# An unequal split of tokens over eight cores, with one program per kind of core behind a branch

## The chip, the cores and the metric

The kernel runs on the 8 cores of one Trainium2 chip, as one launch. Cores 0 to 3 are one die, 4 to 7 the other. Each core has a matrix engine (TensorE, PE), a vector engine (VectorE, DVE), a scalar engine (ScalarE, ACT), GpSimd (POOL) and a sync engine (SyncE, SP), which here does nothing but issue copies (DMAs).

The metric is the device time of the slowest core, in microseconds (us). The three fast runs of the kernel before lie within 0.1% of each other (1601.88 to 1602.89 us), those of the changed kernel within 0.2% (1641.26 to 1644.21). Some executions fall into a slower state in which a die runs at a lower granted clock: the changed kernel had one run of 1760.98 us in which all cores of die 0 were near clock 0.90 (0.883 to 0.904), where its fast runs have 0.958 to 0.983 on that die. A "look" is one profiled execution with its time; a run "with rounds" was also timed in turns with the kernel before, on the same chip.

## The reference

One decoder layer on `x` of shape (2, 4096, 2048). An input projection of 16384 columns gives q, k and v of three groups of 8 attention heads, gates, and the input of a pooling branch. Cut to what matters here:

```python
DILATED_GROUPS = ((128, 1), (512, 4), (2048, 16))   # (window, dilation)
...
for g, (window, dilation) in enumerate(DILATED_GROUPS):
    # query t attends to t, t-d, t-2d, ..., t-window
    o_g, lse_g = dilated_window_attention(qg, kg, v[:, :, g], window, dilation)
...
x = x + jnp.einsum('bsd,de->bse', merged, w_out)
```

Group 2 looks back 2048 tokens. A core that holds a stretch of a sequence therefore needs the keys and values of up to 2048 tokens before it, its *halo*, and computes them itself from x. Groups 0 and 1 need at most the last 512 of these.

## The kernel before

Each sequence is cut into four equal parts, one for each of four cores: 1024 own tokens, 2048 halo tokens. All eight cores run one program. Where the halo lies before the start of the sequence, its x is zero and a mask removes it.

The projections are sums over 16 blocks of 128 input features: matmuls of 128 weight columns against up to 512 tokens. A small scheduler written in Python orders the instructions of all engines when the kernel is built, one list for each engine.

In stage 1 the keys and values of group 2 go through DRAM, because they are needed later, sorted by their position modulo 16. Values are computed in tiles of 128 tokens x 512 columns (4 heads); each tile is copied out of PSUM by ACT, and stored by one copy that SP issues:

```python
def value_tile(qd, t, i):
    vi = yield ("acq", P_vst)                       # one of 3 staging tiles
    yield ("op", "act", act_us(512), lambda a: a.copy(out=vst[vi][:], in_=ps[i][:]), [B_ps[i]], [B_vst[vi]])
    F.release(P_pp, i)
    yield ("dma", "sp", 131e3, lambda s: s.dma_start(
        out=v2d[4 * qd:4 * qd + 4, :, t, :].rearrange("h p c -> p h c"),
        in_=vst[vi][:].rearrange("p (h c) -> p h c", h=4)), [B_vst[vi]], [B_v2d[(qd, t)]], f"vs{vi}")
```

In stage 2, attention, each head's keys and values of group 2 are loaded back:

```python
def load_k2(h, i):
    ...
    ("dma", "sp", 786e3, lambda s: s.dma_start(out=v2[i][:], in_=v2d[h]), ...)
    ("dma", "sp", 786e3, lambda s: s.dma_start(out=k2[i][:], in_=k2d[h]), ...)
```

The rotary embedding of keys and queries needs the two halves of 32 rows swapped. That is done by two small copies on the same SP queue, which here are called the *swap*:

```python
def rope(pool, rots, B_rots, tag, st, B_st, n, tb, B_tb, t0):
    ...
    def swap(hf):
        yield ("dma", "sp", 40e3, lambda s: s.dma_start(
            out=rb[32 + 16 * hf:48 + 16 * hf, 0:n], in_=st[16 - 16 * hf:32 - 16 * hf, 0:n]), ...)
```

Stages 3 to 5 (pooling, gates, output projection) are streams of matmuls with weights loaded by POOL's queue.

## Time and profile before

1602.32 us, the median of three fast runs (1601.88 to 1602.89). The profile:

| what | value | view |
|---|---|---|
| PE busy | 1537.1 us of 1605.8 (96%) | page, part 1 |
| chain that ended last | 92% PE | page, part 4 |
| PE busy, 280 to 1500 us | 1219.95 of 1220 us, clock 1.00 | windows |
| PE busy, 0 to 280 us | 221.51 of 280 us, clock 0.84 | windows |
| first load of x issued | 1.06 us | timeline |

The page of the kernel before, part 2: the span in 40 slices, each digit the busy tenths of one slice, and the granted clock in tenths.

```profile
PE   3699987999999999999999999999999999999997
...
PEclk9778888999999999999999999999999999999999
```

The windows of the slowest core of the kernel before; the columns are the stretch in us, then busy us and number of instructions for PE, weight loads, DVE, ACT and POOL, then clock, DMA share and GB/s.

```profile
0.00:280.00 280.00, 221.51 (x833) 90.79 (x834) 153.32 (x231) 155.86 (x221) 99.94 (x80) 0.84 0.57 146
280.00:1500.00 1220.00, 1219.95 (x6499) 622.34 (x6498) 482.82 (x741) 414.33 (x713) 73.42 (x139) 1.00 0.43 82
```

After the start-up the PE has practically no gap: whatever removes matmul columns there shortens the kernel, as long as nothing new makes the PE wait. The price of a matmul is read from the timeline of PE (core 2; start, duration, then the group):

```profile
512.40 2.76 PE L734 MATMUL ps<-s_hX,s_w_56 128*128 128x384 bf16 x16
515.00 0.33 PE L751 MATMUL ps<-s_sq_50,s_ones 128*128 128x384 bf16 x1
...
525.48 3.62 PE L734 MATMUL ps<-s_hX,s_w_56 128*128 128x512 bf16 x16
528.93 0.38 PE L751 MATMUL ps<-s_sq_50,s_ones 128*128 128x512 bf16 x1
```

From start to start, 16 matmuls of 384 columns take 2.60 us and 16 of 512 take 3.45 us. That is 162.5 and 215.8 ns a matmul, and both fit columns / 2.4 ns plus 2.5 ns.

In the middle of attention (600 to 680 us, core 1) the swap copies of queries land in 1.9 to 2.7 us; the columns are the copy, its count, KB each, and median us from issue to landing:

```profile
s_k_88<-k2d SPq DMA_DIRECT2D x1, 768.0 KB, 4.7
s_v_89<-v2d SPq DMA_DIRECT2D x1, 768.0 KB, 4.8
s_rotb_103<-s_qS_101 SPq DMA_DIRECT2D x4, 32.0 KB, 1.9
...
s_rotb_104<-s_qT_111 SPq DMA_DIRECT2D x2, 32.0 KB, 2.7
```

### The profile page before, as it was taken

To read this page: it belongs to the slowest core of one execution; us is meant where nothing else is said; L and a number is where in the kernel's file an instruction comes from. 1 tells how busy PE (TensorE), PEld (TensorE's weight loads), DVE (VectorE), ACT (ScalarE), POOL (GpSimd) and SP (SyncE) were. 2 spreads that over 40 slices of the span, in tenths; PEclk is the share of its full clock that TensorE was granted. 3 is DMA by queue.
4 is the path that set the end of the run, shared out by engine and by line. 5 is a ranking of instruction groups with operands and counts; after the bars stand their busy time and mean duration, and the time that the engine had idled before them with its cause. 6 is when DMAs were issued, how large, how long until landed. Compare 5 with 4: busy or idle time off the path is not lost.

```text
span 1605.8 us, 23141 instructions; the slowest of 8 cores (1596.8 to 1605.8 us)
## 1 busy us (share of the span) xinstructions
PE 1537.1 (96%) x7772; PEld 756.3 (47%) x7772; DVE 655.5 (41%) x999; ACT 570.2 (36%) x932; POOL 176.5 (11%) x225
## 2 busy tenths in 40 slices
PE   3699987999999999999999999999999999999997
PEld 1234433445645455555555555564444444444443
DVE  5457266423000477675027676675322222221221
ACT  3654476323111556664146665521111111111000
POOL 1033645001000000000000000000000000000000
PEclk9778888999999999999999999999999999999999
DMA  9953532117142644443354443434444444444883
GB/s 204 195 166 107 157 101 87 54 48 144 43 117 47 109 99 91 84 99 80 53 93 84 91 98 63 85 67 94 72 74 77 79 79 76 73 76 79 192 215 106
DMA packets 80468, 158.87 MB, mean 99 GB/s; under 512 B 33824, under 2 KB 41888, under 8 KB 80352
## 3 DMA queue, kind: packets, MB, share of 16 engines
q0 software_dynamic: 23184, 84.42, 31.6%
q1 hardware_dynamic: 56544, 72.51, 14.9%
q8 instruction: 65, 1.06, 0.3%
q10 hardware_dynamic: 624, 0.46, 0.1%
q14 instruction: 51, 0.42, 0.1%
HBM read 216.27 MB, written 20.97 MB: 148 GB/s over the span
## 4 chain that ended last, share of the span: by engine, by line
PE 92%; DMA 2%; issue 2%; DVE 2%; ACT 1%; SPq 0%; DVEq 0%; ACTq 0%
PE ps L734 69%; PE ps L1445 7%; PE ps L1395 7%; PE ps L845 3%; PE ps L751 2%; PE ps L1081 1%; PE ps L1116 1%; PE ps L1120 1%; DMA s_xs_63<-xc 1%; DMA s_rota_78<-s_kst_74 1%; PE ps L678 1%; PE ps L1301 0%; DMA s_rota_78<-s_kst_71 0%; DVE s_acc L674 0%; DMA s_rota_78<-s_kst_72 0%
## 5 line engine op out<-in xcount | busy, mean ns | idle before, releaser
L734 PE MATMUL ps<-s_hX,s_w_56 128*128 128x512 bf16 (+3 forms) x3712 | 801.4, 368 | 0.0
L734 PEld LDWEIGHTS ps<-s_hX,s_w_56 128*128 128x128 bf16 x3712 | 364.1, 98 | 375.7 <-issue 13.3
L578 POOL DMA_DIRECT2D s_w_56<-wst x152 | 80.4, 530 | 1228.0 <-PE ps L734 878.9
L734 PE MATMUL ps<-s_w_56,s_hX 128*128 128x512 bf16 x672 | 147.2, 379 | 0.0
L1445 PE MATMUL ps<-s_mT,s_w_56 128*128 128x512 bf16 x512 | 110.7, 379 | 0.0
L734 PEld LDWEIGHTS ps<-s_w_56,s_hX 128*128 128x128 bf16 x672 | 71.6, 107 | 71.5
L760 DVE SCALAR_TENSOR_TENSOR s_kS_107<-ps,s_cst,s_rr_51 128x384 bf16<-128x384 f32 x8 | 4.9, 615 | 182.7 <-PE ps L734 178.6
L1445 PEld LDWEIGHTS ps<-s_mT,s_w_56 128*128 128x128 bf16 x512 | 50.1, 98 | 60.4
L755 ACT ACTIVATE s_rr_52<-ps 128x512 f32<-128x512 f32 (+1 forms) x72 | 42.6, 591 | 66.7 <-PE ps L751 57.8
L755 ACT ACTIVATE s_rr_51<-ps 128x512 f32<-128x512 f32 (+1 forms) x72 | 41.4, 575 | 68.1 <-PE ps L751 64.7
L734 PE MATMUL ps<-s_w_57,s_hTh_54 128*128 128x512 bf16 x256 | 63.1, 408 | 0.0
L734 PE MATMUL ps<-s_w_57,s_hTh_55 128*128 128x512 bf16 x256 | 61.9, 408 | 0.0
L1395 PE MATMUL ps<-s_pT,s_w_56 128*128 128x512 bf16 x256 | 60.5, 379 | 0.0
L1395 PE MATMUL ps<-s_aT,s_w_56 128*128 128x512 bf16 x256 | 60.5, 379 | 0.0
L748 ACT ACTIVATE s_sq_49<-ps 128x512 bf16<-128x512 f32 (+1 forms) x72 | 42.0, 584 | 40.2 <-PE ps L734 38.7
L734 PE MATMUL ps<-s_w_57,s_hX 128*128 128x512 bf16 x256 | 55.6, 379 | 0.0
L748 ACT ACTIVATE s_sq_50<-ps 128x512 bf16<-128x512 f32 (+1 forms) x72 | 41.7, 580 | 33.7 <-PE ps L734 32.8
L751 PE MATMUL ps<-s_sq_49,s_ones 128*128 128x512 bf16 (+1 forms) x72 | 27.6, 383 | 22.5 <-ACT s_sq_49 L748 21.6
L758 ACT ACTIVATE s_rr_52<-s_rr_52 128x512 f32<-128x512 f32 (+1 forms) x72 | 44.5, 618 | 5.5
L758 ACT ACTIVATE s_rr_51<-s_rr_51 128x512 f32<-128x512 f32 (+1 forms) x72 | 43.6, 606 | 6.1 <-ACT s_rr_51 L755 0.4
L734 PEld LDWEIGHTS ps<-s_w_57,s_hX 128*128 128x128 bf16 x256 | 36.7, 143 | 18.6
L734 PEld LDWEIGHTS ps<-s_w_57,s_hTh_54 128*128 128x128 bf16 x256 | 26.5, 103 | 35.5 <-issue 20.7
(299 smaller groups left out, 1620.1 us busy)
## 6 DMA issues: line engine op xcount, KB each, us to landing
s_w_56<-wst POOLq DMA_DIRECT2D x152, 512.0 KB, 5.2
s_w_57<-wst POOLq DMA_DIRECT2D x8, 512.0 KB, 10.2
s_xs_58<-xc SPq DMA_DIRECT2D x6, 512.0 KB, 5.9
s_xs_59<-xc SPq DMA_DIRECT2D x6, 512.0 KB, 5.6
s_xs_60<-xc SPq DMA_DIRECT2D x6, 512.0 KB, 6.0
s_xs_61<-xc SPq DMA_DIRECT2D x6, 512.0 KB, 7.3
s_xs_62<-xc SPq DMA_DIRECT2D x6, 512.0 KB, 7.6
s_xs_63<-xc SPq DMA_DIRECT2D x6, 512.0 KB, 8.0
```

Of the source, the lines that this page charges most:

```text
L578: yield ("dma", "pool", 1048576, lambda g: g.dma_start(out=wsl[pos][:].rearrange("p k n -> p (k n)"), in_=wst[k]), after, [B_w[pos]], f"w{ ...
L678: yield ("op", "pe", 1.0, lambda t, ax=ax: t.matmul(ps[ax][:], lhsT=onesf[:], rhs=acc[:], start=True, stop=True), [B_acc, B_onesf], [B_ps[ ...
L734: yield ("op", "pe", mm_us(n), lambda t, kc=kc, a=lhs(kc), b=rhs(kc): t.matmul(ps[i][:, 0:n], lhsT=a, rhs=b, start=(kc == 0), stop=(kc == ...
L748: yield ("op", "act", act_us(n), lambda a: a.activation(out=sq[si][:, 0:n], in_=ps[i][:, 0:n], func=AF.Square), [B_ps[i]], [B_sq[si]])
L751: yield ("op", "pe", mm_us(n), lambda t: t.matmul(ps[ax][:, 0:n], lhsT=ones[:], rhs=sq[si][:, 0:n], start=True, stop=True), [B_sq[si], B_o ...
L755: yield ("op", "act", act_us(n), lambda a: a.activation(out=rr[ri][:, 0:n], in_=ps[ax][:, 0:n], func=AF.Ln, bias=float(128 * EPS)), [B_ps[ ...
L758: yield ("op", "act", act_us(n), lambda a: a.activation(out=rr[ri][:, 0:n], in_=rr[ri][:, 0:n], func=AF.Exp, scale=-0.5), [B_rr[ri]], [B_r ...
L845: yield ("op", "pe", mm_us(512), lambda t, kc=kc, b=mov(kc): t.matmul(ps[i][:], lhsT=w["t"][:, kc, :], rhs=b, start=(kc == 0), stop=(kc == ...
L1081: yield ("op", "pe", mm_us(n), lambda t, kap=kap, qap=qap, e0=e0, n=n: t.matmul(ps[si][:, e0:e0 + n], lhsT=kap, rhs=qap, start=True, stop= ...
L1116: yield ("op", "pe", mm_us(n), lambda t, vap=vap, e1=e1, cc=cc, n=n, k=k: t.matmul(nu[:, cc:cc + n], lhsT=vap, rhs=Eb[ei][:, e1:e1 + n], s ...
L1395: b=src[:, h, t0:t0 + n]: t.matmul(ps[yi][:, 0:n], lhsT=a, rhs=b, start=(h == 0), stop=(h == 7)), w["bufs"] + [B_src[h]], [B_ps[yi]])
L1445: b=mT[:, db, t0:t0 + n]: t.matmul(ps[i][:, 0:n], lhsT=a, rhs=b, start=(db == 0), stop=(db == KC - 1)), w["bufs"] + [B_mT[db]], [B_ps[i]])
```

## The change

The first core of a sequence computes 2048 halo tokens that do not exist, the second 1024. The change gives these cores more own tokens and no such halo: 1168 tokens and no halo, 1008 with 1168 halo tokens, and twice 960 with 2048. The program is built three times, and each engine picks its arm by a word loaded from DRAM.

```diff
+KINDS = ((1168, 0), (1008, 1168), (960, 2048))
+KIND = (0, 1, 2, 2)
+START = (0, 1168, 2176, 3136)
...
+        def arms(name, eng):
+            reg = eng.alloc_register("kind_" + name)
+            eng.reg_load(reg, io["kind"])
+            for k in eng.Switch(eng.snap(reg), n=len(KINDS)):
+                runs[k](name, eng)
...
 def value_tile(qd, t, i, nr):
     yield ("dma", "sp", 131e3, lambda s: s.dma_start(
-        out=v2d[4 * qd:4 * qd + 4, :, t, :].rearrange("h p c -> p h c"),
-        in_=vst[vi][:].rearrange("p (h c) -> p h c", h=4)), ...
+        out=v2d[4 * qd:4 * qd + 4, 0:nr, t, :].rearrange("h p c -> p h c"),
+        in_=vst[vi][0:nr].rearrange("p (h c) -> p h c", h=4)), ...
...
 def load_k2(h, i):
+    if H:
+        part(lambda s: s.dma_start(out=k2[i][:, 0:2048].rearrange("p (r l) -> p r l", r=16)[:, :, 0:Hr],
+                                   in_=k2d[h, :, 0:H].rearrange("p (r l) -> p r l", r=16)), ...)
+        part(lambda s: s.dma_start(out=k2[i][:, 2048:2048 + T], in_=k2d[h, :, H:H + T]), ...)
+        part(lambda s: s.dma_start(out=v2[i][0:Hr, 0:16, :], in_=v2d[h, 0:Hr, 0:16, :]), ...)
+    ...
+    part(lambda s: s.dma_start(out=v2[i][0:nr, t0:NV2, :], in_=v2d[h, 0:nr, t0:NV2, :]), ...)
...
```

(Sizes become functions of the kind; matmul pieces follow, 400 tokens instead of 512 and so on.) With 16 positions modulo 16, a value tile of the no-halo core, and a halo tile of the 1008-token core, has 1168 / 16 = 73 rows. The own tiles of the other kinds have 126 and 120 rows, and the halo tiles of the 960-token cores still 128.

## The prediction

> **What bounds the kernel now.** TensorE, by the columns it streams. The page gives PE 96% busy and a chain that is 92% PE. The table of windows gives PE 1219.95 us busy of the 1220 us from 280 to 1500 us, at granted clock 1.00. The loss is elsewhere: before 280 us the PE idles and reruns at a reduced clock (0.75 to 0.87), waiting for x, for the sums of squares (two waits, 32.3 us), and for ACT behind copies of late tokens (8.8 us each); and about 10 us of tail follow the last matmul. In the timeline, 16 matmuls of 512 columns take 3.45 us (215.8 ns each) and 16 of 384 take 2.60 us (162.5 ns): both are columns/2.4 ns + 2.5 ns[...]. Over all matmuls of the program this sums to 1495 us; the other 108 us of 1603 are start and tail.
>
> Every core does the same work, although the first core of each sequence computes keys and values for 2048 halo tokens that do not exist, and the second for 1024 such.
>
> **What the change does, by the same sum over each arm (estimates from those two durations).**
> - 1168 tokens, no halo: 8843 matmuls, 1423 us.
> - 1008 + 1168 halo: 7638 matmuls, 1428 us.
> - 960 + 2048 halo: 7638 matmuls, 1432 us.
>
> The split is well balanced, and the slowest kind saves 1495 - 1432 = 63 us. Only some 3 us of this lie in the first 280 us of the 960-token core (its halo chunks stay 512 columns); the rest lies where the PE has no gap, so nearly all is on the critical path.
>
> Added: each engine loads a word from DRAM and branches into one of three arms. [...] The first x load, now issued at 1.06 us, should come near 5 to 7 us, and everything moves with it: +5 us (a guess). Zero-filling of halo keys on POOL and four reloads per head instead of two lie off the path. Weights are needed faster (one 512 KB block per 6.5 us rather than 6.9), but a block lands in 5.2 us with several in flight and DMA is 44% busy, so it holds. The last stage, with DMA 0.8 busy, will be near 0.85.
>
> **Cores.** The 960-token cores keep today's start-up loss: 1603 - 63 + 5 = 1545. The 1008-token cores have less matmul work to hide the start behind, but shorter loads; same loss assumed: 1540. The no-halo cores have no late copies and perhaps half the loss: about 1490. ACT, DVE and POOL element counts fall or stay in all arms, so they should not take over.
>
> **Predicted: 1544 us**, 8 in 10 between 1524 and 1565. Faster by over 2%: 0.92; within 2%: 0.07; slower: 0.01.
>
> **What would show it.** No-halo cores end 40 us or more before the others; the other six end within 15 us of each other. PE busy near 1470 us on the slowest. No PE gaps from about 280 us on. First DMA issue near 6 us.
>
> **What would make it wrong.** A longer start on the 1008-token core (ACT and DVE chains no longer hidden), new PE gaps in attention from shorter pieces and the single accumulation bank, the last stage hitting DMA limits, a branch that costs tens of us[...].

## More of the kernel before

What the prediction did not look at is the value stores. On core 1 of the kernel before (issue time on SP in ns, min/median/max, and last the time from issue to landing of all copies that touch this tensor):

```profile
L827 SPq DMA_DIRECT2D v2d<-s_vst_75 x16: 360/371/977, 127.5 to 433.6; - x16
...
DMA to landing us min/median/max: 1.9/2.0/12.7
```

A store of 128 rows occupies SP for 0.37 us.

## The result, and the profile after

The changed kernel takes 1643.38 us, the median of its three fast runs (1641.26 to 1644.21), against 1602.32 before. The ratio is 1.0253, 95% interval 1.023 to 1.0277: slower by 2.5%. Executions in which one die ran at a lower clock are left out of the means. (Ratios here are the mean time of one kernel's fast runs over that of the other's in the same rounds, so not quite the ratio of the medians.)

The spans of the cores show at once where to look:

```profile
core 0: 1591.4 us, clock 0.971
core 1: 1632.6 us, clock 0.961
core 2: 1548.5 us, clock 0.983
core 3: 1548.0 us, clock 0.983
core 4: 1588.7 us, clock 0.972
core 5: 1641.7 us, clock 0.959
core 6: 1543.7 us, clock 0.983
core 7: 1548.2 us, clock 0.981
```

The 960-token cores (2, 3, 6, 7) are where the prediction had them (1545). The 1008-token cores (1, 5) are 93 and 102 us later than predicted, the no-halo cores (0, 4) some 100. PE busy on the slowest core is 1470.3 us, near the prediction; the time is in waits. The page of that core (5), part 2, to be held against the one above:

```profile
PE   2576679977999989879999798999999999999997
...
PEclk9788789998999999989999899999999999999999
```

There are more gaps in stage 1 (the first 10 slices), and gaps in attention that were not there before, and the clock dips beside them. The waits of PE on core 1 (who, for whom; us in total, times, longest):

```profile
PE ps L835 <- ACT s_sq_143 L832: 27.1, 2, 16.8
...
PE ps L757 <- POOL s_acc L753: 20.8, 2, 18.0
PE ps L1275 <- DVE s_qT_154 L870: 15.4, 2, 8.6
PE ps L1275 <- DVE s_qT_155 L870: 11.7, 2, 6.1
...
PE ps L1275 <- DVE s_qS_202 L870: 5.1, 1, 5.1
```

The same core of the kernel before has no wait for rope, and this one for POOL:

```profile
PE ps L678 <- POOL s_acc L674: 5.3, 1, 5.3
```

L1275 is the score matmul of attention and L870 the last step of rope: attention waits for rotated queries. L757 (L678 before) waits for sums of squares of x that came late. DVE and POOL wait in their turn; the copies show for what. First the value stores on core 0, where all of them have 73 rows, as in the view above:

```profile
L913 SPq DMA_DIRECT2D v2d<-s_vst_80 x11: 387/3973/4077, 146.8 to 282.2; - x11
L913 SPq DMA_DIRECT2D v2d<-s_vst_81 x11: 233/3946/4105, 162.3 to 290.4; - x11
```

Where such stores follow one another, each holds SP for 4 us, ten times as long as one of 128 rows, though it moves 43% less. That is longer than the 3.45 us of the tile's matmuls, so stores pile up. On core 1 other copies stand between the stores: most stores take SP only 0.3 to 0.4 us, and the hold falls on the copy issued next. SP's timeline in stage 1 shows it; loads of x (L715), issued right after a store, take 4.6 and 5.3 us of SP instead of the 0.33 us that others take:

```profile
144.21 5.25 SPq L715 DMA_DIRECT2D s_xs_160<-xc  x1
...
150.02 0.34 SPq L913 DMA_DIRECT2D v2d<-s_vst_175  x1
150.51 4.61 SPq L715 DMA_DIRECT2D s_xs_161<-xc  x1
```

Then attention, core 1, 640 to 670 us, around a reload, to be held against the four lines before:

```profile
s_k_188<-k2d SPq DMA_DIRECT2D x1, 292.0 KB, 4.7
s_v_189<-v2d SPq DMA_DIRECT2D x1, 292.0 KB
...
s_rotb_204<-s_qT_154 SPq DMA_DIRECT2D x2, 31.5 KB, 14.6
```

The swap issued after the reload lands after 14.6 us, where the same swap (of `s_qT`) took 2.7 before. The DVE waits for it (10.5 us idle at 666 us), and the PE for the DVE (8.6 us idle at 669 us).

### The profile page after: what moved, and what is told of

Same layout as the page of the kernel before. It is cut to its first block, busy times and chain, and to the rows that moved or that the text cites. A ratio compares the mean times of both kernels' runs of the same rounds, so it can differ in the third digit from the quotient of the medians.

```text
span 1641.7 us, 22964 instructions; the slowest of 8 cores (1543.7 to 1641.7 us)
## 1 busy us (share of the span) xinstructions
PE 1470.3 (90%) x7644; PEld 786.1 (48%) x7644; DVE 599.7 (37%) x999; ACT 534.8 (33%) x924; POOL 153.7 (9%) x231
## 4 chain that ended last, share of the span: by engine, by line
PE 75%; DMA 9%; SPq 7%; issue 3%; DVE 3%; ACT 1%; POOL 1%; ACTq 0%; DVEq 0%; POOLq 0%
PE ps L818 56%; PE ps L1619 7%; PE ps L1569 7%; SPq L857 3%; SPq L913 2%; DMA s_rotb_204<-s_qT_154 2%; DMA s_rotb_203<-s_qT_155 2%; PE ps L1275 2%; PE ps L1301 1%; SPq L903 1%; PE ps L835 1%; DMA s_rotb_203<-s_qS_202 1%; POOL s_acc L753 1%; PE ps L1305 1%; DMA s_rota_179<-s_kst_171 1%
## 5 line engine op out<-in xcount | busy, mean ns | idle before, releaser
L818 PE MATMUL ps<-s_w_156,s_hX 128*128 128x512 bf16 (+2 forms) x672 | 147.1, 379 | 0.0
L818 PEld LDWEIGHTS ps<-s_w_156,s_hX 128*128 128x128 bf16 (+2 forms) x672 | 82.5, 123 | 60.8
L1619 PE MATMUL ps<-s_mT,s_w_156 128*128 128x496 bf16 (+1 forms) x512 | 109.0, 376 | 0.0
L839 ACT ACTIVATE s_rr_144<-ps 128x512 f32<-128x512 f32 (+3 forms) x72 | 38.0, 528 | 92.2 <-PE ps L835 65.1
L1569 PE MATMUL ps<-s_aT,s_w_156 128*128 128x512 bf16 (+1 forms) x256 | 59.6, 376 | 0.0
L1569 PE MATMUL ps<-s_pT,s_w_156 128*128 128x512 bf16 (+1 forms) x256 | 59.6, 376 | 0.0
L818 PE MATMUL ps<-s_w_157,s_hX 128*126 128x512 bf16 x256 | 59.5, 394 | 0.0
L818 PEld LDWEIGHTS ps<-s_w_157,s_hX 128*126 128x126 bf16 x256 | 59.2, 323 | 0.3
L839 ACT ACTIVATE s_rr_145<-ps 128x512 f32<-128x512 f32 (+3 forms) x72 | 38.8, 539 | 59.1 <-PE ps L835 52.9
L818 PE MATMUL ps<-s_w_157,s_hTh_147 128*73 128x512 bf16 x256 | 57.8, 383 | 0.0
L818 PE MATMUL ps<-s_w_157,s_hTh_148 128*73 128x512 bf16 x256 | 57.3, 384 | 0.0
L757 PE MATMUL ps<-s_acc,s_onesf 128*128 128x292 f32 (+2 forms) x12 | 7.9, 762 | 53.9 <-DVE s_acc L753 35.0
L832 ACT ACTIVATE s_sq_142<-ps 128x512 bf16<-128x512 f32 (+3 forms) x72 | 38.1, 529 | 39.2 <-PE ps L818 38.3
L832 ACT ACTIVATE s_sq_143<-ps 128x512 bf16<-128x512 f32 (+3 forms) x72 | 38.4, 534 | 32.9 <-PE ps L818 30.0
## 6 DMA issues: line engine op xcount, KB each, us to landing
s_w_157<-wst POOLq DMA_DIRECT2D x8, 512.0 KB, 10.5
```

The lines of the kernel that those rows point to most:

```text
L818: yield ("op", "pe", mm_us(n), lambda t, kc=kc, a=lhs(kc), b=rhs(kc): t.matmul(ps[i][0:nr, 0:n], lhsT=a, rhs=b, start=(kc == 0), stop=(kc ...
L832: yield ("op", "act", act_us(n), lambda a: a.activation(out=sq[si][:, 0:n], in_=ps[i][:, 0:n], func=AF.Square), [B_ps[i]], [B_sq[si]])
L839: yield ("op", "act", act_us(n), lambda a: a.activation(out=rr[ri][:, 0:n], in_=ps[ax][:, 0:n], func=AF.Ln, bias=float(128 * EPS)), [B_ps[ ...
L1569: b=src[:, h, t0:t0 + n]: t.matmul(ps[yi][:, 0:n], lhsT=a, rhs=b, start=(h == 0), stop=(h == 7)), w["bufs"] + [B_src[h]], [B_ps[yi]])
L1619: b=mT[:, db, t0:t0 + n]: t.matmul(ps[i][:, 0:n], lhsT=a, rhs=b, start=(db == 0), stop=(db == KC - 1)), w["bufs"] + [B_mT[db]], [B_ps[i]])
```

## Experiments

**Theory A.** A copy of 73 rows is served by a single DMA engine out of 16, and so takes longer than one of 128 rows that is spread over them. Which other row counts would be quick or slow was the author's estimate, and the runs below test it. No view names the engines of a copy, but the consequences can be tested, and the packets of the kept traces bear on it (after before_64_64 below). From 204 to 232 us SP of core 0 issues nothing but these stores; its queue then (packets, MB, share of 16 engines' time):

```profile
q1 hardware_dynamic: 1987, 0.51, 8.0%
```

That is 18 GB/s, and 8.0% of 16 engines is 1.3 engines (never more than two packets overlap). An estimate: 73 KB in 4.07 us is 18.4 GB/s, so by theory A the 292 KB of a reload of 73 rows would keep one engine busy for 16 us, close to the 14.6 us of the swap behind it.

**Theory B.** The key reload of the 1008-token cores writes 16 pieces of 146 bytes in each partition, 2048 small pieces, and these delay the swaps.

**Theory C.** It has nothing to do with copies: these cores have less matmul work to hide the start behind, and the shorter pieces make attention's chains longer. This was the prediction's own worry.

All runs gave correct results but the two marked as wrong. A span can differ between fast runs of the same program by some 10 us (core 1 of the changed kernel: 1632.6, 1637.2 and 1642.6; core 5 only 1638.5 to 1641.7), so differences below that are not read. Gains below are counted from the look at the changed kernel, whose core 1 is the lowest of the three.

### split_all: 73 rows as 64 and 9, stores and reloads

```diff
+def row_parts(n):
+    return [(0, 64), (64, 73)] if n == 73 else [(0, n)]
...
-    s.dma_start(out=v2d[4 * qd:4 * qd + 4, 0:nr, t, :]..., in_=vst[vi][0:nr]...)
+    for r0, r1 in row_parts(nr):        # each with its own semaphore
+        s.dma_start(out=v2d[4 * qd:4 * qd + 4, r0:r1, t, :]..., in_=vst[vi][r0:r1]...)
...                                      # both value reloads in load_k2 in the same way
```

> Every 73-row copy of values (stores to DRAM in stage 1, reloads in stage 2, on the no-halo and the 1008-token cores) is issued as 64 rows and 9 rows; nothing else changes. Theory A (a copy of 73 rows is served by one DMA engine of the 16, so it holds the sync queue and the rope swaps behind it): the 1008-token cores fall from 1633-1642 us to 1550 (+-15), the no-halo cores from 1590 to about 1520, the 960-token cores stay at 1544-1549, and the program takes about 1550 us, faster than before by some 3%. A store no longer takes 4 us on the sync queue. Theory B (146-byte pieces of the key reload delay the swaps): the store part gains something at most, attention gaps (33 us) remain on the 1008-token cores, nothing moves much: 1610 or more. Theory C (less matmul work to hide the start behind, shorter attention pieces): no change, 1635-1645 us.

1558.07 us median against 1602.14 before: ratio 0.971 (0.966 to 0.976), **faster by 2.9%**. The 1008-token cores took 1555.2 and 1556.2 us, the no-halo cores 1535.6 and 1535.1, the others 1542.5 to 1550.3. The stores of core 1, and then its longest waits of PE:

```profile
L927 SPq DMA_DIRECT2D v2d<-s_vst x80: 308/607/1046, 113.4 to 406.1; - x80
```

```profile
PE ps L764 <- DVE s_acc L760: 33.5, 2, 26.3
PE ps L842 <- ACT s_sq L839: 28.9, 5, 10.1
PE ps L952 <- DVE s_hTh L795: 11.1, 5, 3.8
PE ps L764 <- POOL s_acc L760: 7.2, 2, 4.4
```

No store occupies SP for over 1.05 us, and the waits of attention for rope (the three of L1275 above, 32 us) are gone; the queries' swaps at 640 to 670 us land in 2.1 us. Theory C falls as the cause of this loss: the matmul pieces are unchanged here. The windows of PE on core 1 divide the gain; first the changed kernel, then split_all:

```profile
0.00:410.00 410.00, 291.26 (x1464) 0.90 0.42 98
410.00:1100.00 690.00, 657.02 (x3730) 0.98 0.39 73
```

```profile
0.00:410.00 410.00, 327.02 (x1619) 0.93 0.45 103
410.00:1100.00 690.00, 688.22 (x3938) 1.00 0.44 80
```

36 us of PE time come back in stage 1 (327.02 - 291.26) and 31 us in attention (688.22 - 657.02), and the mean clock is higher in both (0.93 after 0.90, 1.00 after 0.98), where there are fewer gaps.

### split_stores and split_loads: one half of it each

The same edit, for the stores alone and for the reloads alone.

> Only the stores of 73 rows are split into 64 and 9; the reloads stay. Theory A: the part of the loss before 410 us goes, about 50 us of the 1008-token cores (to about 1590) and 45 us of the no-halo cores (to about 1545); the gaps of attention between 500 and 1100 us stay. Theories B and C: unchanged within 10 us.

1607.3 us. Core 1 took 1605.7 us (27 less than in the changed kernel), core 0 1568.8 (23 less). The direction is as theory A has it, the sizes are about half of what was expected, and the attention gaps stay as expected. The waits for rope stay (26.3 and 11.7 us on core 1), and swaps after a reload land after 7 to 10 us in the median.

> Only the reloads of 73 rows are split; the stores stay. Theory A: the swaps that follow a reload land in 2 to 4 us and no longer in 14.6, the attention gaps (33 us of PE idle on the 1008-token cores, 26 us on the no-halo cores) go, and the cores end some 35 and 30 us sooner: 1600 and 1560. Theory B: the no-halo cores, which have no 146-byte pieces, gain; the 1008-token cores do not.

1593.79 us. Core 1 took 1591.6 us (41 less), core 0 1553.9 (37 less): somewhat more than expected. No wait for rope is left on core 1, and the queries' swaps land in 2.0 to 2.4 us; the late sums of squares stay (POOL 20.6 us). The 1008-token cores gain although their 146-byte pieces are still there, which speaks against theory B. So the reloads cost more than the stores on all four cores (0 and 4, 1 and 5), the reverse of what was expected; together they account for 68 of the 77 us that split_all wins on core 1.

### k2_compact: theory B by itself

```diff
-    s.dma_start(out=k2[i][:, 0:2048].rearrange("p (r l) -> p r l", r=16)[:, :, 0:Hr], in_=k2d[h, :, 0:H]...)
+    s.dma_start(out=k2[i][:, 0:H], in_=k2d[h, :, 0:H])
...
-    ks[:, 128 * (r + 8 * bb):128 * (r + 8 * bb) + 128]
+    ks[:, Hr * (r + 8 * bb):Hr * (r + 8 * bb) + 128]      # the mask removes what lies past Hr
```

> The key reload of the 1008-token cores is made contiguous (2336 bytes a partition instead of 16 pieces of 146 bytes); the 73-row copies stay. Theory A: the 1008-token cores gain less than 8 us and the swap behind a reload still takes over 10 us. Theory B: the swap lands in 2 to 4 us and the 1008-token cores gain 30 to 40 us (to about 1600). The other cores are the same program, so unchanged in both.

1645.3 us, cores 1 and 5 at 1643.6 and 1643.4: nothing gained. The waits for rope on core 1 are 33.1 and 5.2 us, and the swap behind a reload (640 to 680 us) is as late as ever:

```profile
s_k<-k2d SPq DMA_DIRECT2D x1, 292.0 KB, 4.4
...
s_rotb<-s_qT SPq DMA_DIRECT2D x2, 31.5 KB, 16.1
```

Theory B falls.

### both_fixed: the small pieces again, without the 73-row copies

split_all and k2_compact together.

> The 64+9 rows of split_all and the contiguous key reload together. With the one-engine copies gone, theory B is asked again for what is left of it: if the 146-byte pieces still delay anything on the path, the 1008-token cores gain 5 us or more over split_all (1555-1556 us); if not, less than 3 us, and the program stays at 1553-1558 us. Either way faster than before by about 3%.

1555.99 us median, ratio 0.9713 (0.9696 to 0.9729), the 1008-token cores at 1553.5 and 1554.5 us: some 2 us under those of split_all, which ran on another chip. The small pieces cost nothing that can be told apart here.

### split_71_2: a control

```diff
-    return [(0, 64), (64, 73)] if n == 73 else [(0, n)]
+    return [(0, 71), (71, 73)] if n == 73 else [(0, n)]
```

> A control for split_all: the same two copies in place of one, with the same semaphores and order, but cut 71 + 2 instead of 64 + 9. [...] theory A says that the large part stays on one engine and nothing is won: the 1008-token cores 1625-1650 us, the no-halo cores 1585-1600. If the gain of split_all came from having two copies, or from the changed schedule, it comes here too: about 1556.

1654.85 us, cores 1 and 5 at 1653.2 and 1645.4, cores 0 and 4 at 1601.1 and 1594.6, two of the four by up to 3 us above theory A's ranges. Two copies, the same semaphores, the same order of issue, and nothing is won. So the gain of split_all is neither the second copy nor a luckier schedule. One store held SP for 19.8 us.

### split_62_11: a dose

`(0, 62), (62, 73)`.

> The dose: the 73-row copies cut 62 + 11, [...] with the same number of copies in each case. Theory A: [...] most of the loss goes: the 1008-token cores between 1560 and 1580 us. If any row number that is no multiple of 16 were as bad as 73, about 1645.

1568.11 us, cores 1 and 5 at 1565.3 and 1566.4. Most of the loss is gone, and some 10 us more are left than with 64 + 9 (four runs of split_all: 1555.2 to 1557.3 on these cores), among them 6 us of waits for rope on core 1. That most of the loss would go was the author's estimate; on core 1 the stores of both parts held SP for 0.43 us in the median and 4.46 us at most. Between large parts of 71 rows (1653), 62 (1565) and 64 (1555) the number of rows alone was changed, and the time of core 1 falls as the 4-byte packets that a pair of copies sends rise (3, 13 and 25, counted below). The three ran on three chips, on which the kernel before took 1602 us each time.

### t1152: other constants, no copy split

```diff
-KINDS = ((1168, 0), (1008, 1168), (960, 2048))
+KINDS = ((1152, 0), (1024, 1152), (960, 2048))
-START = (0, 1168, 2176, 3136)
+START = (0, 1152, 2176, 3136)
```

> The changed kernel with other constants only: 1152 tokens without halo, 1024 with 1152 halo tokens, twice 960 with 2048. Rows per value tile become 72 (no halo, and halo of the second core) and 128 (own tiles of the second core); no copy is split. Theory A [...] no store takes 4 us on the sync queue; the columns of the 1024-token cores sum to 1443 us against 1428, so those cores should take 1556 + 15 = 1571 us, the no-halo cores 1535 - 22 = 1513, the 960-token cores 1544-1550. If what counts is any row number that is not a multiple of 16, or the small halo itself (theory C), the 1024-token cores stay above 1630 us.

1565.3 us median, ratio 0.9768 (0.9752 to 0.9785): faster by 2.3%, from three constants. Cores 1 and 5: 1563.4 and 1564.1; no-halo: 1512.2 and 1510.0. No store of core 0 holds SP for over 0.54 us:

```profile
L913 SPq DMA_DIRECT2D v2d<-s_vst x32: 292/292/542, 145.6 to 258.0; - x32
```

72 rows are no multiple of 16 and hold SP no longer than 128 did (0.29 us in the median, against 0.37 on core 1 of the kernel before), so a multiple of 16 is not needed. The 1024-token cores took 7 us less than the 1571 that were expected. The balance of columns is worse than with 1168, and still it beats the changed kernel by 78 us.

### before_73_55 and before_64_64: the same fault put into the kernel before

```diff
+    for r0, r1 in [(0, 73), (73, 128)]:      # before_64_64: [(0, 64), (64, 128)]
         s.dma_start(out=v2d[4 * qd:4 * qd + 4, r0:r1, t, :]..., in_=vst[vi][r0:r1]...)
```

> The kernel before, with each of its 48 stores of 128 value rows issued as 73 + 55 rows; nothing else. Theory A: each 73-row part takes about 4 us on the sync queue or holds what follows it by that much, more than the 3.45 us of matmuls per value tile, so stage 1 of every core grows by 30 to 70 us and the program to 1630-1670 us. If the loss of the changed kernel comes from anything else in it, this stays within 5 us of 1602 (an issue costs 0.4 us more).

1652.78 us in its fast run, the cores at 1644.9 to 1650.9: slower by 47 to 52 us on all eight than the medians of the kernel before on that chip, with 48 stores changed and nothing else.

> The control for before_73_55: each of the 48 stores of the kernel before as 64 + 64 rows[...]. Theory A: within 5 us of 1602 (two issues of 0.35 us in place of one lie off the path). If two stores per tile cost the time by themselves, 1640 or more as with 73 + 55.

1603.8 us. Two stores per tile cost nothing that can be told apart (the kernel before took 1601.84 us on that chip); it is where the cut lies. Core 1 of the two, before_73_55 first:

```profile
L832 SPq DMA_DIRECT2D v2d<-s_vst x96: 218/2013/14131, 124.6 to 501.8; - x96
```

```profile
L832 SPq DMA_DIRECT2D v2d<-s_vst x96: 574/595/1637, 124.2 to 438.8; - x96
```

The packets of the traces were counted when this document was checked, and not predicted. SP's queue carries packets of 4 bytes beside those of the rows. A store of 128 rows that has the queue to itself (kernel before, core 0, from 164.93 us) is 512 packets of 256 bytes and 16 of 4 bytes, of which up to 22 overlap, and it lands in 2.0 us. From 204 to 232 us, where core 0 of the changed kernel issues 7 stores of 73 rows, there are 7 of 4 bytes, one a store, and never more than two packets overlap. Over the whole program on core 0 the count of 4-byte packets is 4552 in the changed kernel; the other runs differ from it, or from the 6432 of the kernel before:

| run | 4-byte packets more | copies changed | more for each |
|---|---|---|---|
| split_stores | 768 | 32 stores: 64 + 9 rows, for 73 | 24 |
| split_loads | 192 | 8 reloads: 64 + 9 rows, for 73 | 24 |
| split_all | 960 | 40 copies: 64 + 9 rows, for 73 | 24 |
| split_62_11 | 480 | 40 copies: 62 + 11 rows, for 73 | 12 |
| split_71_2 | 80 | 40 copies: 71 + 2 rows, for 73 | 2 |
| t1152 | 440 | 40 copies: 72 rows, for 73 | 11 |
| before_73_55 | -192 | 48 stores: 73 + 55 rows, for 128 | -4 |
| before_64_64 | 768 | 48 stores: 64 + 64 rows, for 128 | 16 |

With 1 for a copy of 73 rows and 16 for one of 128, that makes 25 for 64 + 9, 13 for 62 + 11, 3 for 71 + 2, 12 for 72, 12 for 73 + 55 and 32 for 64 + 64. That such a packet stands for one engine of a copy is theory A's reading: two packets at once against 22 agree with it, and no run here shows what else could give these numbers. What in the row count sets the number was not shown.

### all960_switch and all960_straight: the branch

All cores take the arm of 960 + 2048 tokens (so the output is wrong, and holds NaN, in both), once through the switch and once without it.

```diff
-            reg = eng.alloc_register("kind_" + name)
-            eng.reg_load(reg, io["kind"])
-            for k in eng.Switch(eng.snap(reg), n=len(KINDS)):
-                runs[k](name, eng)
+            runs[2](name, eng)
```

> All eight cores are sent into the arm of 960 + 2048 tokens (the output of four of them is wrong on purpose), through the switch. It isolates the arm that holds no 73-row copy. All cores should take 1540-1552 us, as the 960-token cores do beside the others.

1553.74 us, the median of its three fast runs (1550.89 to 1554.35; the fourth, 1679.09 us, was slow), cores at 1542.6 to 1552.2.

> The same program on all eight cores without the load of the kind and without the switch (wrong on purpose in the same way). The prediction guessed 5 us for the branch, and the first load of x is issued at 6.6 us with it and at 1.1 us without: if that delay carries through, this takes 5 to 7 us less than all960_switch. If the start hides it, less than 2 us[...].

1542.27 us median (1541.7 to 1543.06), cores at 1535.1 to 1540.7. The branch costs about 11 us, not 5 (11.5 by the medians of the fast runs, 10.7 by their means). On core 1, the first load of x and the first projection matmul, with the switch and then without:

```profile
6.80 37.49 SPq L715 DMA_DIRECT2D s_xs<-xc  x15
...
35.53 9.84 PE L932 MATMUL ps<-s_hTh,s_w 128*128 128x512 bf16 x38 [2.54 <-DVE s_hTh L788]
```

```profile
1.06 38.78 SPq L712 DMA_DIRECT2D s_xs<-xc  x16
...
29.75 15.27 PE L929 MATMUL ps<-s_hTh,s_w 128*128 128x512 bf16 x59 [2.95 <-DVE s_hTh L785]
```

The first load is issued 5.7 us later. The first projection matmul comes later by 8 us in the median of the cores (36.5 against 28.4 us), and the cores scatter more (32.5 to 38.8, against 27.9 to 29.8), of which the slowest counts. From 300 to 1500 us PE is busy all 1200 us in both (cores 1 and 5), so nothing is paid in that stretch, though the loss is over 10 us. What delays the start beyond the 5.7 us was not taken apart.

## Why the prediction was wrong

- *TensorE bounds the kernel by its columns, and the price is columns/2.4 ns + 2.5 ns.* Right. Without the branch, eight cores of 960 tokens took 1542.27 us (all960_straight), against 1603 - 63 = 1540. That the 960-token cores hit 1545 beside the others (1543.7 to 1548.5) is helped by luck, since the branch cost 11 us and not 5. So is the PE busy time of the slowest core, 1470.3 us against "near 1470": that was meant for a 960-token core, and these had 1457 to 1461; the 1008-token core has 1470 at a lower clock (0.959), and 1459 in split_all. The 2.5 ns come from the 215.8 and 162.5 ns of the trace.
- *"Zero-filling of halo keys on POOL and four reloads per head instead of two lie off the path", and "same loss assumed: 1540" for the 1008-token cores.* This is the step that failed. I counted copies by number and bytes and never by their rows. The stores of 73 rows held SP, on themselves or on the copy behind, for 4 us each, and the reloads held the swap behind them for 15 us, and so came onto the path: 36 us of PE time in stage 1 and 31 us in attention on core 1, with the mean clock down from 0.93 to 0.90 and from 1.00 to 0.98. The causal chain is shown by split_all (the loss goes), split_71_2 (it stays with two copies), and before_73_55 (it comes in the kernel before). Zero-filling on POOL was not the cause of this loss: split_all leaves it as it is.
- *"No PE gaps from about 280 us on"* and *"the other six end within 15 us of each other"* failed for that reason. With split_all the six ended within 13.7 us (1542.5 to 1556.2), and the program took 1558 us, inside the range predicted. The 1008-token cores were still 15 us over their 1540. The branch, 6 us dearer than guessed, can account for that much; the rest, which may be the longer start that the prediction feared, was not taken apart.
- *"The no-halo cores ... perhaps half the loss: about 1490."* Wrong in a second way. With the copies mended they took 1535 us, 112 us over their 1423 us of matmuls, against 108 before: the loss was not halved at all. Their start shows a DMA share of 0.84 and 0.94 in the first two stretches of 40 us, and their PE ran at clock 0.70 and 0.84 from 40 to 120 us; that the loads of x and weights bound it was not tested. It did not matter for the total.
- *"+5 us (a guess)" for the branch.* Off in size: about 11 us. The prediction was right that the first load would be issued near 5 to 7 us (an estimate of the author's): it came at 6.80 us in all960_switch, 5.7 later than in all960_straight (1.06). That delay holds the load of the kind and the switch, and the two were not parted. The prediction took that delay for the whole cost.
- *What would make it wrong* named the symptoms, a longer start of the 1008-token core and new gaps in attention, but put them down to chains of ACT and DVE and to shorter pieces. As the cause of the 77 us that split_all wins back on core 1 that is refuted, since split_all changes neither; of the 15 us that stay it is open.

## What to carry to other kernels

When a change makes a tile's row count a function of the problem, check the row count of every copy, not its bytes: in this case 73 rows in one copy, issued in a row, cost ten times the queue time of 128 (4.0 us against 0.37), and 72 (0.29) or 64 + 9 (0.58 for a part, core 0 of split_all) did not. Copies "off the path" are so only while they keep pace: what shares their queue (here the swap of the rotary embedding, 14.6 us behind a reload where 2.7 was the time before) is on the path. Where one core of eight is late, look at the cores' spans first; that the cores of one kind hit the prediction while the others did not told which numbers to compare.
